# An encoder's feed-forward input projections: one moving operand of 512 columns from the high and low parts of x, halves added afterwards

## The chip, the cores and the metric

The kernel runs on one core of a Trainium2 chip. The metric is the device time of one execution in microseconds, the median of the runs; lower is better. Five engines work in parallel, each through its own queue in order: PE (matrix multiply), DVE (vector), ACT (scalar and activation), POOL and SP (which issues the DMAs here).

## The reference, cut

An encoder of two layers over 256 tokens of 1024 features. Each layer is a mixer (two kinds of attention and a short convolution, gated), a cross attention to a memory of 256 tokens, and a feed-forward part with a convolution over tokens in its gate; each ends in a residual and a layer norm. All is in fp32. The feed-forward part is

```python
def conv_ffn(x, ffn_w_in, ffn_conv_w, ffn_conv_b, ffn_w_out):
    u, gt = jnp.split(x @ ffn_w_in, 2, axis=-1)      # 1024 -> 2 x 2816
    a = dwconv(gt, ffn_conv_w) + ffn_conv_b          # 3 taps over the tokens
    return (jax.nn.silu(a) * u) @ ffn_w_out
```

## The kernel before, in words

Every fp32 product is made of three matmuls on fp32r operands: both factors are split into a high part (ACT casts it) and a low part (DVE subtracts the cast from the source), in `split_from` (L249); `mm3` (L243) multiplies high by high, high by low and low by high into one PSUM bank, so L245, L246 and L247 carry nearly all of PE's time.

The weights come as 355 units of 512 KB. `prefetch` (L1089) brings each by DMA into a `raw` tile and splits it into a `hi` and a `lo` tile of 128x1024, seven units ahead of their use (LOOK); eight pairs of tiles exist (WB). A unit of the input projections holds 8 blocks of 128x128 for one block of 128 output features, and `proj_f8` (L263) runs 8 x 3 matmuls with the weights stationary and 256 tokens of x moving. x lies in four tiles named big, two for high and two for low parts (class `Act`); `ln` fills them at the end of a layer norm: PE transposes x by 128x128 (L414) into a PSUM bank of the kind `att`, and `split_from` splits it.

PSUM has eight banks of 512 columns: three `acc` and five `att`. The feed-forward input, `ffn_in` (L1013), runs over 22 blocks f of 128 features. A block has a unit for up and one for gate; both write one acc bank, columns 0 to 255 and 256 to 511. ACT and DVE then apply the convolution (L1039, L1040, L1042), the silu (L1044) and the product with up (L1045) straight from the bank, and the result is split for `ffn_out`. In layer 1 the up parts of the first four blocks are computed earlier, tokens on the partitions, by `up_first` (L1003), while x's second half is still being normalized; for these blocks (`f < ready`) only a gate unit is run and the stored up is transposed into the same bank (L1029).

`Encoder.interleave` plans the steps of the main chain and the steps that fill its waits; from the planned program a tile scheduler sets the order of the instructions on each engine, so that a change of the instructions can change the order around it. Splits behind a layer norm are marked urgent, and weight splits are held behind them. SP's queue carries the DMAs in program order. In the rows, names are of the program: `hi` and `lo` a unit's weights, `big` the tiles of x or of the memory, `fa` the gate's tile in SBUF, `ident` the identity for a transposition.

Of the kernel before, what the change touches and what calls it, by code (L numbers as in the profile page):

```python
# [20 lines left out]
F32R = mybir.dt.float32r  # L21
# [4 lines left out]
P = 128  # L26
D = 1024
KT = 8
# [57 lines left out]
class Step:  # L86
# [5 lines left out]
    def __init__(self, fn, cost=0.0, lat=0.0, units=(), acq=0, rel=0, fill=0):  # L92
        self.fn, self.cost, self.lat, self.units = fn, cost, lat, list(units)
        self.acq, self.rel, self.fill = acq, rel, fill
# [97 lines left out]
        return self.los[k // self.per][:, k % self.per, a:b]  # L192


def rd(t):
    return t.bitcast(F32)


class Encoder:
# [63 lines left out]
    def proj_f8(self, u, xa, o):  # L263

        hi, lo = (t.rearrange("p (k c) -> p k c", k=KT) for t in u)
        for k in range(KT):
            self.mm3(o, hi[:, k], lo[:, k], xa.hi(k), xa.lo(k), k == 0, k == KT - 1)

    def proj_m2(self, u, xa, kt, i, o, first, last):

# [89 lines left out]
    def ln(self, i, nxt, rel, pre=2.6):  # L360
# [46 lines left out]
        def transp(h):  # L407
            nc, n = self.nc, w // P
            if i == 0 and h == 0:
                self.T[nxt] = self.act_tile()  # L410
            a = self.T[nxt]
            pt = self.att()[:, :w].rearrange("p (k t) -> p k t", k=n)
            for k in range(n):
                nc.tensor.transpose(pt[:, k], self.x[i][:, (n * h + k) * P:(n * h + k + 1) * P], self.ident)  # L414
            t, k = n * h // 4, n * h % 4
            for ins in self.split_from(pt, a.his[t][:, k:k + n, i * P:(i + 1) * P],
                                       a.los[t][:, k:k + n, i * P:(i + 1) * P]):
                self.urgent(ins)

        yield Step(norm, 0, pre, rel=rel)  # L420
# [39 lines left out]
    def load_mem(self, then=None):  # L460

        n = 1024 if then is None else 512
        hi, lo = [self.big(F32R) for _ in range(2)], [self.big(F32R) for _ in range(2)]
        for j in range(2 * 1024 // n):
            raw = self.raw() if then is None else self.t512()
            t = j * n // 1024
            for m in range(0, n, 256 if then is not None and j == 0 else n):
                w = 256 if then is not None and j == 0 else n
                sl = slice(j * n % 1024 + m, j * n % 1024 + m + w)
                self.nc.sync.dma_start(raw[:, m:m + w], self.aps["memT"][:, j * n + m:j * n + m + w])  # L470
                self.split_from(raw[:, m:m + w], hi[t][:, sl], lo[t][:, sl])
                if then is not None:
                    then(j, m)
        self.T["mem"] = Act([t.rearrange("p (k t) -> p k t", k=4) for t in hi],
                            [t.rearrange("p (k t) -> p k t", k=4) for t in lo])

    def raw(self):
        return self.wp.tile([P, 1024], F32, tag="raw", name=self.nm("raw"), bufs=4)
# [534 lines left out]
    def ffn_in(self, l, xn, ready=0):  # L1013
        T = self.T
        for f in range(NF):
            st = {}

            def up(u, f=f, st=st):
                st["o"] = self.acc()
                self.proj_f8(u, T[xn], st["o"][:, 0:256])  # L1020

            def gate(u, f=f, st=st):
                nc = self.nc
                if f < ready:
                    st["o"] = self.acc()
                self.proj_f8(u, T[xn], st["o"][:, 256:512])
                if f < ready:
                    for i in range(NT):
                        nc.tensor.transpose(st["o"][:, i * P:(i + 1) * P], T["um", i][:, f * P:(f + 1) * P],  # L1029
                                            self.ident)  # L1030
                if f == 0:
                    T["hT"] = Act([self.big4(F32R)], [self.big4(F32R)])
                elif f % 4 == 0:
                    T["hT"].his.append(self.big4(F32R))
                    T["hT"].los.append(self.big4(F32R))
                w = self.fcw[:, l, f]
                ug = st["o"].rearrange("p (j t) -> p j t", j=2)
                t = self.tmp.tile([P, S], F32, tag="fa", name=self.nm("fa"), bufs=3)
                nc.scalar.activation(t, ug[:, 1], AF.Identity, bias=w[:, 3:4], scale=w[:, 1:2])  # L1039
                nc.vector.scalar_tensor_tensor(out=t[:, 1:], in0=ug[:, 1, :S - 1], scalar=w[:, 0:1], in1=t[:, 1:],  # L1040
                                               op0=ALU.mult, op1=ALU.add)
                nc.vector.scalar_tensor_tensor(out=t[:, :S - 1], in0=ug[:, 1, 1:], scalar=w[:, 2:3],  # L1042
                                               in1=t[:, :S - 1], op0=ALU.mult, op1=ALU.add)
                nc.scalar.activation(t, t, AF.Silu)  # L1044
                nc.vector.tensor_tensor(out=t, in0=t, in1=ug[:, 0], op=ALU.mult)  # L1045
                self.split_from(t, T["hT"].hi(f), T["hT"].lo(f))
            if f >= ready:
                yield Step(up, U, units=[("fu", l, f)])
            yield Step(gate, U, units=[("fg", l, f)])
# [171 lines left out]
```

## Time and profile before

| | us |
|---|---|
| time, median of 3 runs | 1135.65 (1134.47 to 1135.9) |
| the profiled execution | 1135.06 |
| its span, first to last instruction | 1133.3 |
| PE busy in the span | 1103.8 (97%) |
| DVE busy | 798.9 (70%) |
| ACT busy | 612.7 (54%) |
| granted clock of PE, mean | 0.994 |

The span is one execution seen by the profiler; 1.8 us of the execution's time lie around it. Busy time of PE contains waits that pipelining hides, so the distance between the starts of two matmuls tells more than their durations. The idle time in brackets behind a row of a timeline is that of the engine just before it, and the name behind the arrow is what ended it.

### The profile page before, as it was taken

How to read it: one execution, taken by the hardware profiler on the slowest of the kernel's cores; microseconds unless marked ns; L12 is line 12 of the kernel's file. 1: busy time of each engine (PE TensorE's matmuls, PEld its weight loads, DVE VectorE, ACT ScalarE, POOL GpSimd, SP SyncE). 2: the span in 40 equal slices, each digit the busy share in tenths (PEclk: the TensorE clock that was granted, in tenths of full speed). 3: DMA queues.
4: the chain of work that ended last, by engine and by line, in shares of the span. 5: the costliest groups of instructions: out<-in, count | busy, mean ns of one | idle time of the engine just before them, and what ended most of it. 6: DMA issues, size and time to landing. Idle time of an engine off the chain costs nothing.

```text
span 1133.3 us, 18595 instructions
## 1 busy us (share of the span) xinstructions
PE 1103.8 (97%) x7340; PEld 1014.8 (90%) x7340; DVE 798.9 (70%) x1198; ACT 612.7 (54%) x958; POOL 12.4 (1%) x18
## 2 busy tenths in 40 slices
PE   7999999999999999999999999999999979999997
PEld 6899998888898999998889999888889879999986
DVE  6788888666864876665586888865787576666644
ACT  5556767445453565554445667744536436555540
POOL 0000000000000000000000000000000000000001
PEclk9999999999999999999999999999999989999999
DMA  8785437567563666565747544556746444665551
GB/s 297 245 262 170 136 135 232 183 189 241 168 186 99 200 204 186 182 181 189 263 143 231 174 148 167 179 185 197 256 145 201 140 149 150 186 185 180 182 180 37
DMA packets 60471, 208.53 MB, mean 184 GB/s; under 512 B 7008, under 2 KB 8288, under 8 KB 60384
## 3 DMA queue, kind: packets, MB, share of 16 engines
q1 hardware_dynamic: 59952, 206.83, 56.9%
q8 instruction: 57, 0.93, 0.3%
q10 hardware_dynamic: 432, 0.52, 0.1%
q14 instruction: 30, 0.25, 0.1%
HBM read 204.18 MB, written 1.05 MB: 181 GB/s over the span
## 4 chain that ended last, share of the span: by engine, by line
PE 66%; DVE 3%; ACT 1%; DMA 1%; issue 1%; DVEq 0%; ACTq 0%; SPq 0%
PE acc L245 18%; PE acc L246 18%; PE acc L247 18%; PE att L246 3%; PE att L247 3%; PE att L245 3%; DMA raw<-in_w_dram 1%; DVE lo L251 1%; PE att L414 0%; ACT hi L250 0%; DVE s L355 0%; DVE big L251 0%; PE att L617 0%; PE att L851 0%; PE att L1003 0%
## 5 line engine op out<-in xcount | busy, mean ns | idle before, releaser
L251 DVE TENSOR_TENSOR lo<-raw,hi 128x1024 fp32r<-128x1024 f32 x355 | 431.8, 1222 | 237.1 <-ACT hi L250 235.6
L250 ACT CAST hi<-raw 128x1024 fp32r<-128x1024 f32 x355 | 370.7, 1050 | 333.1 <-PE acc L246 155.5
L245 PE MATMUL acc<-big,hi 128*128 128x256 f32 x1376 | 391.0, 285 | 3.1 <-ACT big L294 1.2
L246 PE MATMUL acc<-big,hi 128*128 128x256 f32 x1376 | 390.2, 284 | 1.9 <-DVE big L251 1.9
L247 PE MATMUL acc<-big,lo 128*128 128x256 f32 x1376 | 390.2, 284 | 0.6 <-DVE lo L251 0.6
L245 PEld LDWEIGHTS acc<-big,hi 128*128 128x128 f32 x1376 | 263.3, 192 | 5.1 <-ACT big L294 1.8
L246 PEld LDWEIGHTS acc<-big,hi 128*128 128x128 f32 x1376 | 263.6, 192 | 3.0 <-DVE big L251 2.6
L247 PEld LDWEIGHTS acc<-big,lo 128*128 128x128 f32 x1376 | 263.6, 192 | 1.2 <-DVE lo L251 1.1
L245 PE MATMUL acc<-hi,big 128*128 128x512 f32 x584 | 230.1, 396 | 6.1 <-ACT hi L250 6.0
L246 PE MATMUL acc<-lo,big 128*128 128x512 f32 x584 | 230.8, 395 | 0.5 <-DVE lo L251 0.5
L247 PE MATMUL acc<-hi,big 128*128 128x512 f32 x584 | 228.0, 393 | 0.0
L245 PEld LDWEIGHTS acc<-hi,big 128*128 128x128 f32 x584 | 110.5, 190 | 27.1 <-ACT hi L250 6.5
L247 PEld LDWEIGHTS acc<-hi,big 128*128 128x128 f32 x584 | 110.7, 190 | 23.0
L246 PEld LDWEIGHTS acc<-lo,big 128*128 128x128 f32 x584 | 110.9, 190 | 21.2 <-DVE lo L251 1.2
L246 PE MATMUL att<-lo,big 128*128 128x256 f32 (+1 forms) x228 | 72.6, 319 | 0.0
L245 PE MATMUL att<-hi,big 128*128 128x256 f32 (+1 forms) x228 | 72.4, 318 | 0.0
L247 PE MATMUL att<-hi,big 128*128 128x256 f32 (+1 forms) x228 | 72.3, 318 | 0.0
L250 ACT CAST big<-att 128x512 fp32r<-128x512 f32 (+2 forms) x64 | 28.1, 458 | 45.8 <-PE att L247 25.8
L251 DVE TENSOR_TENSOR big<-att,big 128x512 fp32r<-128x512 f32 (+2 forms) x64 | 32.1, 518 | 27.7 <-ACT big L250 27.2
L245 PEld LDWEIGHTS att<-hi,big 128*128 128x128 f32 x228 | 43.3, 190 | 4.9
L246 PEld LDWEIGHTS att<-lo,big 128*128 128x128 f32 x228 | 43.3, 190 | 4.5
L247 PEld LDWEIGHTS att<-hi,big 128*128 128x128 f32 x228 | 43.3, 190 | 3.1
(145 smaller groups left out, 948.2 us busy)
## 6 DMA issues: line engine op xcount, KB each, us to landing
raw<-in_w_dram SPq DMA_DIRECT2D x355, 512.0 KB, 4.0
t<-in_bias_dram SPq DMA_DIRECT2D x16, 256.0 KB, 5.5
big<-in_ln_g_dram SPq DMA_DIRECT2D x6, 512.0 KB, 5.5
big<-in_ln_b_dram SPq DMA_DIRECT2D x6, 512.0 KB, 6.2
raw<-in_memT_dram SPq DMA_DIRECT2D x6, 512.0 KB, 4.4
big<-big SPq DMA_DIRECT2D x16, 128.0 KB, 2.3
x<-in_x_dram SPq DMA_DIRECT2D x4, 256.0 KB, 7.9
t<-in_memT_dram SPq DMA_DIRECT2D x3, 256.0 KB, 7.9
```

The lines of the kernel that those rows point to most:

```text
L245: mm(o, lh, rh, start=first, stop=False)
L246: mm(o, lh, rl, start=False, stop=False)
L247: mm(o, ll, rh, start=False, stop=last)
L250: return (self.nc.scalar.copy(ah, src), self.nc.vector.tensor_tensor(out=al, in0=src, in1=rd(ah), op=ALU.subtract))
L251: self.nc.vector.tensor_tensor(out=al, in0=src, in1=rd(ah), op=ALU.subtract))
```

## The change

The tiles of x behind every layer norm, and those of the memory, get a new layout (class `Twin`): each of the four tiles holds two blocks of 128 features, for each the 256 tokens of the high part and beside them the 256 of the low part. Splits are made two blocks at a time, so a transposition of 512 columns takes two casts and two subtractions where it took one of each.

In the feed-forward input, `proj_twin` takes the place of `proj_f8`: with a high weight stationary it moves high and low part of x in one matmul of 512 columns, and with a low weight the high part alone, 256 columns. The first wide matmul opens the bank, the eight with low weights follow in one run, then the other seven wide ones. The bank's two halves must be added: `fold` copies the second half to SBUF on ACT and adds the first on DVE. So up and gate have a bank each, which is free after the fold, and convolution and product read SBUF. In layer 1's first four blocks the transposed up goes to an acc bank of its own, which the product reads.

```diff
+class Twin:
+    def __init__(self, tiles):
+        self.tiles = [t.rearrange("p (k h t) -> p k h t", k=2, h=2) for t in tiles]
+    def hi(self, k, a=0, b=S):
+        return self.tiles[k // 2][:, k % 2, 0, a:b]
+    def lo(self, k, a=0, b=S):
+        return self.tiles[k // 2][:, k % 2, 1, a:b]
+    def both(self, k):
+        return self.tiles[k // 2][:, k % 2].rearrange("p h t -> p (h t)")
+    def put(self, split, src, k, a=0, b=S):
+        out, n = [], src.shape[1]
+        for j in range(k, k + n, 2):
+            m = min(2, n)
+            t = self.tiles[j // 2][:, j % 2:j % 2 + m]
+            got = split(src[:, j - k:j - k + m], t[:, :, 0, a:b], t[:, :, 1, a:b])
+            out += got or ()
+        return out
...
+    def proj_twin(self, u, xa):
+        mm, o = self.nc.tensor.matmul, self.acc()
+        hi, lo = (t.rearrange("p (k c) -> p k c", k=KT) for t in u)
+        mm(o, hi[:, 0], xa.both(0), start=True, stop=False)
+        for k in range(KT):
+            mm(o[:, S:], lo[:, k], xa.hi(k), start=False, stop=False)
+        for k in range(1, KT):
+            mm(o, hi[:, k], xa.both(k), start=False, stop=k == KT - 1)
+        return o
+    def fold(self, dst, o):
+        self.nc.scalar.copy(dst, o[:, S:])
+        self.nc.vector.tensor_tensor(out=dst, in0=o[:, :S], in1=dst, op=ALU.add)
...
-                self.T[nxt] = self.act_tile()
+                self.T[nxt] = Twin([self.big(F32R) for _ in range(4)])
...
-            t, k = n * h // 4, n * h % 4
-            for ins in self.split_from(pt, a.his[t][:, k:k + n, i * P:(i + 1) * P],
-                                       a.los[t][:, k:k + n, i * P:(i + 1) * P]):
+            for ins in a.put(self.split_from, pt, n * h, i * P, (i + 1) * P):
                 self.urgent(ins)
...
             def up(u, f=f, st=st):
-                st["o"] = self.acc()
-                self.proj_f8(u, T[xn], st["o"][:, 0:256])
+                st["ug"] = self.t512().rearrange("p (j t) -> p j t", j=2)
+                self.fold(st["ug"][:, 0], self.proj_twin(u, T[xn]))
+                st["up"] = st["ug"][:, 0]
...
                 if f < ready:
-                    st["o"] = self.acc()
-                self.proj_f8(u, T[xn], st["o"][:, 256:512])
+                    st["ug"] = self.t512().rearrange("p (j t) -> p j t", j=2)
+                self.fold(st["ug"][:, 1], self.proj_twin(u, T[xn]))
                 if f < ready:
+                    st["up"] = self.acc()[:, 0:256]
                     for i in range(NT):
-                        nc.tensor.transpose(st["o"][:, i * P:(i + 1) * P], T["um", i][:, f * P:(f + 1) * P],
+                        nc.tensor.transpose(st["up"][:, i * P:(i + 1) * P], T["um", i][:, f * P:(f + 1) * P],
...
-                ug = st["o"].rearrange("p (j t) -> p j t", j=2)
+                ug = st["ug"]
...
-                nc.vector.tensor_tensor(out=t, in0=t, in1=ug[:, 0], op=ALU.mult)
+                nc.vector.tensor_tensor(out=t, in0=t, in1=st["up"], op=ALU.mult)
```

`load_mem` fills a `Twin` in the same way, through `put`. The line numbers of the changed file are higher by 26 to 41: `split_from` stands on L276 and L277, `proj_twin` on L299 to L303, `fold` on L307 and L308, the transposition of up on L1067.

PE, one unit of layer 0's feed-forward input in the steady part, before (the first 6 of 24 matmuls):

```order
L245 MATMUL acc_4183<-big_3930,hi_3955 128x256
L246 MATMUL acc_4183<-big_3932,hi_3955 128x256
L247 MATMUL acc_4183<-big_3930,lo_3956 128x256
L245 MATMUL acc_4183<-big_3930,hi_3955 128x256
L246 MATMUL acc_4183<-big_3932,hi_3955 128x256
L247 MATMUL acc_4183<-big_3930,lo_3956 128x256
```

and in the changed program (the whole unit; x2 is two matmuls of the same row):

```order
L299 MATMUL acc_4428<-big_3941,hi_4211 128x512 [waits DVE_49]
L301 MATMUL acc_4428<-big_3941,lo_4212 128x256 x2
L301 MATMUL acc_4428<-big_3942,lo_4212 128x256 x2
L301 MATMUL acc_4428<-big_3943,lo_4212 128x256 x2
L301 MATMUL acc_4428<-big_3944,lo_4212 128x256 x2
L303 MATMUL acc_4428<-big_3941,hi_4211 128x512
L303 MATMUL acc_4428<-big_3942,hi_4211 128x512 x2
L303 MATMUL acc_4428<-big_3943,hi_4211 128x512 x2
L303 MATMUL acc_4428<-big_3944,hi_4211 128x512 x2
```

24 matmuls became 16, those with the low weights stand together behind the first, and the unit waits for DVE (its bank).

PE, layer 1, between the gates of the second and the third block (t is the stored up), before:

```order
L247 MATMUL acc_9925<-big_9739,lo_9651 128x256
L1029 MATMUL acc_9925<-ident,t_9837 128x128
L1029 MATMUL acc_9925<-ident,t_9874 128x128
L245 MATMUL acc_9966<-big_9738,hi_9662 128x256
L246 MATMUL acc_9966<-big_9740,hi_9662 128x256
L247 MATMUL acc_9966<-big_9738,lo_9663 128x256
```

and in the changed program, at the same place:

```order
L303 MATMUL acc_9738<-big_9553,hi_9462 128x512 x2
L1067 MATMUL acc_9757<-ident,t_9653 128x128 [waits DVE_49]
L1067 MATMUL acc_9757<-ident,t_9690 128x128
L299 MATMUL acc_9775<-big_9550,hi_9474 128x512 [waits DVE_49]
L301 MATMUL acc_9775<-big_9550,lo_9475 128x256 x2
L301 MATMUL acc_9775<-big_9551,lo_9475 128x256 x2
```

The transposed up went to the gate's own bank and now goes to another, for which it waits, and the next gate waits for a bank too.

DVE, layer 0, where x is split for the cross attention's query projection (att: the transposed x; big_288 and big_289: the memory's keys), before:

```order
L251 TENSOR_TENSOR lo_3075<-raw_3072,hi_3074 128x1024 [waits DMAHW6_49,Activation_49]
L251 TENSOR_TENSOR lo_3113<-raw_3110,hi_3112 128x1024 [waits DMAHW7_49,Activation_49]
L251 TENSOR_TENSOR big_3050<-att_3141,big_3048 128x2x128 [waits Activation_49]
L251 TENSOR_TENSOR lo_3149<-raw_3146,hi_3148 128x1024 [waits DMAHW0_49,Activation_49]
L251 TENSOR_TENSOR big_3195<-big_289,big_3193 128x1024 [waits Activation_49]
L251 TENSOR_TENSOR big_3050<-att_3177,big_3048 128x2x128 [waits Activation_49]
L251 TENSOR_TENSOR big_3051<-att_3182,big_3049 128x2x128 [waits Activation_49]
L251 TENSOR_TENSOR big_3051<-att_3187,big_3049 128x2x128 [waits Activation_49]
```

and in the changed program:

```order
L277 TENSOR_TENSOR lo_3085<-raw_3082,hi_3084 128x1024 [waits DMAHW6_49,Activation_49]
L277 TENSOR_TENSOR big_3058<-att_3113,big_3058 128x2x128 [waits Activation_49]
L277 TENSOR_TENSOR big_3056<-att_3153,big_3056 128x2x128 [waits Activation_49]
L277 TENSOR_TENSOR big_3057<-att_3189,big_3057 128x2x128 [waits Activation_49]
L277 TENSOR_TENSOR big_3058<-att_3194,big_3058 128x2x128 [waits Activation_49]
L277 TENSOR_TENSOR big_3059<-att_3199,big_3059 128x2x128 [waits Activation_49]
L277 TENSOR_TENSOR big_3059<-att_3113,big_3059 128x2x128 [waits Activation_49]
L277 TENSOR_TENSOR lo_3125<-raw_3122,hi_3124 128x1024 [waits DMAHW7_49,Activation_49]
L277 TENSOR_TENSOR lo_3161<-raw_3158,hi_3160 128x1024 [waits DMAHW0_49,Activation_49]
L277 TENSOR_TENSOR big_3206<-big_288,big_3204 128x1024 [waits Activation_49]
```

One weight split (`lo` from `raw`) stands ahead of x's pieces where two stood, the pieces of x follow one another, and the splits from big_288 and big_289 come behind them.

## Rows read from the trace of the kernel before

**Rows 1.** The page: engines (busy us, share of span, instructions); the chain that ended last.

```profile
PE 1103.8 (97%) x7340; PEld 1014.8 (90%) x7340; DVE 798.9 (70%) x1198; ACT 612.7 (54%) x958; POOL 12.4 (1%) x18
...
PE 66%; DVE 3%; ACT 1%; DMA 1%; issue 1%; DVEq 0%; ACTq 0%; SPq 0%
```

**Rows 2.** The page, costliest groups: busy us, mean ns of one, idle time before.

```profile
L245 PE MATMUL acc<-big,hi 128*128 128x256 f32 x1376 | 391.0, 285 | 3.1 <-ACT big L294 1.2
...
L245 PEld LDWEIGHTS acc<-big,hi 128*128 128x128 f32 x1376 | 263.3, 192 | 5.1 <-ACT big L294 1.8
```

**Rows 3.** Timeline of PE, layer 0, feed-forward: start us, duration us, line, operation.

```profile
439.79 0.28 PE L245 MATMUL acc<-big,hi 128*128 128x256 f32 x1
...
442.67 0.28 PE L245 MATMUL acc<-big,hi 128*128 128x256 f32 x1
```

**Rows 4.** Windows: us, busy of PE, PEld, DVE, ACT, POOL, PEclk, DMA, GB/s.

```profile
440.00:460.00 20.00, 20.00 (x169) 20.00 (x168) 13.83 (x22) 11.16 (x19) 0.00 (x0) 1.00 0.59 184
300.00:304.00 4.00, 2.36 (x18) 1.88 (x18) 4.00 (x7) 3.26 (x7) 0.00 (x0) 1.00 0.20 36
928.00:932.00 4.00, 1.50 (x7) 1.53 (x8) 4.00 (x10) 0.68 (x2) 0.00 (x0) 0.50 0.75 252
```

**Rows 5.** Timeline of PE, layer 0, where 512 and 256 columns are mixed.

```profile
519.89 0.40 PE L245 MATMUL acc<-hi,big 128*128 128x512 f32 x1
520.12 0.40 PE L246 MATMUL acc<-lo,big 128*128 128x512 f32 x1
520.36 0.39 PE L247 MATMUL acc<-hi,big 128*128 128x512 f32 x1
...
521.73 0.39 PE L247 MATMUL att<-hi,big 128*128 128x512 f32 x1
521.96 0.28 PE L245 MATMUL att<-hi,big 128*128 128x256 f32 x1
...
522.67 0.40 PE L245 MATMUL acc<-hi,big 128*128 128x512 f32 x1
```

**Rows 6.** Timeline of ACT, first feed-forward blocks of layer 1.

```profile
954.65 1.28 ACT L1044 ACT_TABLE_LOAD   x1
955.94 0.42 ACT L1044 ACTIVATE fa<-fa 128x256 f32<-128x256 f32 x1
...
957.20 0.40 ACT L250 CAST big<-fa 128x256 fp32r<-128x256 f32 x1
```

**Rows 7.** Timeline of DVE, same stretch.

```profile
956.39 0.42 DVE L1045 TENSOR_TENSOR fa<-fa,acc 128x256 f32<-128x256 f32 x1 [0.57 <-ACT fa L1044]
956.73 0.48 DVE L1042 SCALAR_TENSOR_TENSOR fa<-acc,fcw,fa 128x255 f32<-128x255 f32 x1
```

**Rows 8.** Timeline of PE, same stretch (in brackets: idle before, released by).

```profile
956.08 0.38 PE L1029 MATMUL acc<-ident,t 128*128 128x128 f32 x2
956.87 0.39 PE L245 MATMUL acc<-big,hi 128*128 128x256 f32 x1 [0.40 <-DVE fa L1045]
```

**Rows 9.** Timeline of PE at three starts behind a layer norm.

```profile
301.65 0.62 PE L245 MATMUL acc<-big,hi 128*128 128x256 f32 x3 [0.29 <-ACT big L250]
...
303.84 0.39 PE L246 MATMUL acc<-big,hi 128*128 128x256 f32 x1 [1.35 <-DVE big L251]
...
306.44 0.39 PE L246 MATMUL acc<-big,hi 128*128 128x256 f32 x1 [0.20 <-DVE big L251]
...
387.25 0.62 PE L245 MATMUL acc<-big,hi 128*128 128x256 f32 x3 [0.33 <-ACT big L250]
...
930.50 1.09 PE L414 MATMUL att<-ident,x 128*128 128x128 f32 x4 [6.20 <-DVE x L378]
```

**Rows 10.** Timeline of DVE at the first of them.

```profile
301.10 2.35 DVE L251 TENSOR_TENSOR lo<-raw,hi 128x1024 fp32r<-128x1024 f32 x2
303.37 0.42 DVE L251 TENSOR_TENSOR big<-att,big 128x256 fp32r<-128x256 f32 x1
```

More of the change, by code (lines that the diff above doesn't have):

```diff
@@ L462, in load_mem @@
         n = 1024 if then is None else 512
-        hi, lo = [self.big(F32R) for _ in range(2)], [self.big(F32R) for _ in range(2)]
+        mem = Twin([self.big(F32R) for _ in range(4)])
         for j in range(2 * 1024 // n):
             raw = self.raw() if then is None else self.t512()
-            t = j * n // 1024
             for m in range(0, n, 256 if then is not None and j == 0 else n):
                 w = 256 if then is not None and j == 0 else n
-                sl = slice(j * n % 1024 + m, j * n % 1024 + m + w)
                 self.nc.sync.dma_start(raw[:, m:m + w], self.aps["memT"][:, j * n + m:j * n + m + w])
-                self.split_from(raw[:, m:m + w], hi[t][:, sl], lo[t][:, sl])
+                mem.put(self.split_from, raw[:, m:m + w].rearrange("p (k t) -> p k t", t=S), (j * n + m) // S)
                 if then is not None:
                     then(j, m)
-        self.T["mem"] = Act([t.rearrange("p (k t) -> p k t", k=4) for t in hi],
-                            [t.rearrange("p (k t) -> p k t", k=4) for t in lo])
+        self.T["mem"] = mem
     def raw(self):
```

## The prediction, made before the run

> **What bounds the kernel now.** The engine table comes first [rows 1]: PE is busy 97% of the span, DVE 70%, ACT 54%, and two thirds of the chain that ended last is PE. So the end moves with PE's work and with the few places where PE stands still. The costliest groups [rows 2] say what that work is: 128x256 matmuls, 1376 on L245 and as many on L246 and L247; the weight loads beside them (0.19 us) are hidden, since the matmuls follow one another in less. Their own duration (0.28 us) is latency: what one costs is the distance between two starts. In the feed-forward part [rows 3] that is 0.12 us without a gap: a unit starts at 439.79, the next, 24 matmuls later, at 442.67, so 2.88 us. All through those stretches PE is 20.00 of 20 us busy at clock 1.00, DVE 13.83, ACT 11.16 [rows 4]: nothing waits. A unit is worth its PE time there, as long as nothing new waits.
>
> **Part 1: fewer, longer matmuls.** Each changed unit replaces 24 matmuls of 256 columns by 8 of 512 (x's high part and low part beside each other, under the same high weights) and 8 of 256. The columns are the same, so the gain is whatever a matmul costs beyond its columns. Elsewhere the kernel runs 128x512 matmuls mixed with 128x256 ones, like the new unit [rows 5]: from 519.89 to 521.73 eight starts apart take 1.84 us (0.23 each), and the six of 256 columns from 521.96 take 0.71 us to 522.67, so eight take 0.95. A unit becomes 1.84 + 0.95 = 2.79 us, 0.09 less. There are 84 such units (2 x 22 in layer 0, 18 up and 22 gate in layer 1): **−7.5 us**, and I take −7.4. Bounds: with 0.24 for two of the eight wide ones (520.12 to 520.36 is such a gap) and 0.12 for each narrow one a unit is 6 x 0.23 + 2 x 0.24 + 0.96 = 2.82 and the gain 5.0 us; with 0.228 for the wide ones (520.36 to 521.73 are six gaps) and 0.95 for the narrow ones it is 2.77 and the gain 9.2. The Trainium skill, "TensorE: Matmul & The Clock Gate", section "Wait — 56ns, not 53.3ns?", gives start-to-start as columns over 2.4 GHz plus about 2.5 ns; by that the estimate of the gain is 84 x 8 x 2.5 ns = 1.7 us only. The rows disagree: two of 256 columns take 0.24, one of 512 takes 0.23 or less, 10 to 12 ns a pair. It is a rival below.
>
> **Part 2: the additions.** Each unit now ends in an ACT copy of one half of the bank to SBUF and a DVE addition. Nearest rows: an ACT pass over 128x256 takes 0.40 us [rows 6], a DVE pass of that shape that reads PSUM 0.42 [rows 7], in a queue about 0.34 each. DVE's work for a unit was 13.83 / 20 x 2.88 = 1.99 us and becomes some 2.36 of 2.79 (85%), ACT's 1.61 becomes 1.95 (70%). Both fit. The next wait they could cause is PE's for an accumulation bank: there are three, one unit each, so the addition has until the end of the second unit after, 5.6 us. Ahead of it in DVE's order stand at most one weight split (1.22), two convolution steps, a product and a split of 0.4 to 0.5 each: some 2.9 us. So the additions cost nothing in the steady part; if that cover were gone they would cost up to 0.8 us a unit.
>
> **Part 3: layer 1's first four blocks.** Here no up unit lies between the gates, because up was computed earlier; the transposed up goes now to a bank of its own, held until the product at the end of the block. Three banks serve gate, up, gate, up, and each new unit must wait for something that was not in its way before. Before, the third gate waited once, 0.40 us, for the product of the first block [rows 8]; that product is late because ACT loads a table (1.28 us) ahead of the silu [rows 6]. I walk the new order from these times. The second gate's matmuls end near 952.75, its transposes follow. The third gate needs the second's bank: drain of the last matmul (0.16, its 0.28 or so less one start), copy 0.40, addition 0.42, two hand-overs of 0.06 (the product ends at 956.81, PE starts at 956.87 [rows 7, 8]): stall **1.07**. The fourth gate, wanted at 956.9, needs the bank of the second block's up, so that block's product. Behind the table load come the first silu, its product (956.42), on DVE two steps of 0.48 for the second block, a silu of 0.41 and the product of 0.42: ready 958.48, stall **1.58**. The fifth block's up, wanted at 961.4, needs the fourth gate's bank, so copy and addition again: **1.0**. Then two units a block return and the slack with them. Sum 3.65, less the 0.40 that goes: **+3.25 us**. Bounds: 2.0, if the last of the three has passed before PE comes, and 5.0, if one weight split of 1.22 us stands ahead of an addition. The clock is no further cost: an idle stretch of 1.35 us left it at 1.00, 6.2 us of idle time were followed by 0.50 [rows 4, 9].
>
> **Part 4: the starts behind a layer norm.** All layer-norm outputs take the new layout, and a transposition of 512 columns is split in two pieces: one more instruction on ACT and one on DVE, twice a layer norm, about 0.16 us each, all before the other token half's norm and in DVE time that is not yet waited for. But the scheduler's order shifts. At layer 0's cross-attention query projection PE waits 0.29 and 1.35 us [rows 9], because the low part of x (303.37) stands behind two weight splits (301.10 to 303.45) on DVE [rows 10]. In the changed order one split stands ahead and the memory's split has moved behind the four pieces of x: the low part is ready some 1.2 to 1.5 us sooner, and the three pieces behind follow at once. Of 1.84 us of idle time there (0.29, 1.35, and 0.20 at 306.44) I take **−1.5**; bounds 0 and −1.84. At layer 0's feed-forward start PE waits 0.33 us for ACT [rows 9]; there the first unit's second matmul now needs all the columns of both halves, and the last transposition waits for a split to free its bank: **+0.2**, bounds 0 and 0.8. The remaining starts (mixer, layer 1's query projection) change their order by a piece or two in either direction: 0, bounds −1 and +1.
>
> **Sum.** −7.4 + 3.25 − 1.5 + 0.2 = −5.45 on the profiled execution's 1135.06: 1129.6. The median of the runs, 1135.65, stands 0.6 above it, so **1130.1** for the median.
>
> **The rivals.**
> A: a 512-column matmul costs two of 256. For it: single gaps of 0.24 in rows 5, twice 0.12. Against it: the run of eight takes 1.84, not 1.92. Gain 0, the other terms stay: 1135.65 + 1.95 = 1137.6; with the page's 1.7 us, 1135.9.
> B: the banks cost more at layer 1's start, because an addition stands behind a weight split each time and the waits feed on one another (each late product delays the next gate, whose addition is then later): 3 x 1.22 more than the walk, 7 us. For it: DVE is in order and splits are 1.22. Against it: the order puts two of the additions before the split. 1130.1 + 3.7 = 1133.8.
> C: the walk is too dark: ACT and DVE get ahead there, one stall of the three stays, 1.0 less the 0.40. 1130.1 − 2.6 = 1127.5, with the best bound of part 1 1125.7.
> D, slower than before: DVE becomes the bound of the steady part. Its 2.36 us a unit would have to stretch past 2.88, by 22%, through PSUM reads that PE, ACT and DVE share or through waits for silu that block it in order. From there every 0.1 us a unit is 8.4 us: at 2.98 the part loses 8.4 instead of gaining 7.4, 1130.1 + 15.8 = 1145.9. Against it: DVE runs now at 69% there without such stretching, its splits at 1.22 as anywhere.
>
> **How the numbers follow.** Forecast 0.56, C 0.17, B 0.13, A 0.06, D 0.04, other shifts of order 0.04. The range: the bounds of part 1 (−9.2, −5.0) with those of part 3 (2.0, 5.0) and part 4 reach from 1125.6 to 1137.4; leaving out 2 in 10, half on each side, gives 1126.3 to 1134.6. A measurement here can tell about 0.2% (2.3 us) from no change, so faster means under 1133.4: the forecast nearly whole, C, and a part of B: 0.78. Within 0.2%: the rest of B, most of A and of the shifts: 0.14. Slower, over 1137.9: D, the dark part of A, and a part of the shifts: 0.08.
>
> **What would show it.** Right: in the feed-forward stretches the first matmuls of successive units 2.77 to 2.82 us apart, PE 20 of 20 us busy, DVE near 17 and ACT near 14; three idle times of PE of 1.0 to 1.6 us near 950 to 960, put down to DVE's addition and product; one idle time at 302 under 0.5 us. Wrong: units at 2.88 (A), PE idle at the start of units with DVE full (D), idle time at 950 to 960 of 6 us or more (B) or 1 us (C), or new waits at a place that the walk left at nothing, the mixers' starts above all.

## The result and the profile after

The changed kernel takes 1126.68 us, median of 4 runs (1125.99 to 1127.0); the kernel before, in 4 runs beside it, 1135.11 (1134.47 to 1135.9). The ratio is 0.9933, interval 0.9917 to 0.9949: faster by 0.7%. The forecast was 1130.1, its range 1126.3 to 1134.6. The time lies inside, 0.4 us above the range's lower end.

The page of the changed kernel, engines and chain (columns as in [rows 1]):

```profile
PE 1094.9 (97%) x6668; PEld 978.2 (87%) x6668; DVE 833.2 (74%) x1300; ACT 643.4 (57%) x1060; POOL 12.4 (1%) x18
...
PE 92%; DVE 3%; ACT 2%; DMA 1%; issue 1%; SPq 0%; DVEq 0%; ACTq 0%
```

PE has 8.9 us less work, DVE 34 more, ACT 31 more, and the span (1125.1 us) is 8.1 shorter. In the feed-forward part of layer 0 the timeline of PE reads (an entry with x8 is eight matmuls; start us, us, line, operation):

```profile
440.95 0.39 PE L299 MATMUL acc<-big,hi 128*128 128x512 f32 x1
441.18 1.11 PE L301 MATMUL acc<-big,lo 128*128 128x256 f32 x8
442.13 1.78 PE L303 MATMUL acc<-big,hi 128*128 128x512 f32 x7
443.75 0.39 PE L299 MATMUL acc<-big,hi 128*128 128x512 f32 x1
```

From one unit's first matmul to the next it is 2.80 us, and over 40 units in a row 2.793 (they start within 0.002 us of that), where [rows 3] show 2.88. The stretch from 440 to 460 us, columns as in [rows 4]:

```profile
440.00:460.00 20.00, 20.00 (x115) 17.56 (x114) 16.44 (x28) 13.80 (x26) 0.00 (x0) 1.00 0.62 192
```

PE still waits for nothing there, with DVE at 16.44 of 20 us and ACT at 13.80.

The span can be cut where x's first transposition stands behind each layer norm (lines L414 before, L455 after). The lengths of these stages, worked out from the starts of those rows and of the last matmul (the first stage counts from PE's first matmul, 4.5 to 4.7 us into the span), for the kernel before, the changed one, its repetition on another chip, and four experiments told of below:

| stage, us | before | after | again | e4 | e7 | e3 | e1 |
|---|---|---|---|---|---|---|---|
| start to first layer norm | 23.97 | 23.56 | 21.74 | 22.04 | 22.38 | 21.95 | 23.19 |
| mixer, layer 0 | 263.91 | 263.86 | 263.89 | 263.92 | 263.92 | 263.91 | 264.04 |
| cross attention, layer 0 | 90.63 | 88.48 | 88.49 | 88.50 | 89.03 | 88.49 | 88.49 |
| feed-forward, layer 0 | 194.13 | 190.43 | 190.43 | 193.88 | 194.15 | 190.43 | 193.96 |
| mixer, layer 1 | 261.59 | 261.07 | 261.07 | 261.06 | 261.29 | 261.06 | 261.09 |
| cross attention, layer 1 | 91.68 | 91.45 | 91.44 | 91.45 | 91.67 | 91.44 | 91.44 |
| feed-forward, layer 1 | 194.24 | 193.25 | 193.30 | 194.38 | 194.11 | 189.85 | 197.79 |

The middle stages of the changed kernel repeat to 0.03 us, so differences of 0.2 us there are the program's. The first stage differs by 2 us between executions, whatever the kernel, and the traces show with what: in the profiles of before, after and e1 (23.97, 23.56, 23.19) a stretch between 11 and 17 us of the span has a granted clock of 0.50, in the four others (21.74 to 22.38) none has.

Layer 1's first blocks, PE's timeline (in brackets the idle time before, and what ended it):

```profile
945.21 0.38 PE L1067 MATMUL acc<-ident,t 128*128 128x128 f32 x2
946.29 0.50 PE L299 MATMUL acc<-big,hi 128*128 128x512 f32 x1 [0.70 <-DVE t L308]
...
949.21 0.38 PE L1067 MATMUL acc<-ident,t 128*128 128x128 f32 x2
951.01 0.50 PE L299 MATMUL acc<-big,hi 128*128 128x512 f32 x1 [1.42 <-DVE fa L1083]
...
953.92 0.38 PE L1067 MATMUL acc<-ident,t 128*128 128x128 f32 x2
955.01 0.50 PE L299 MATMUL acc<-big,hi 128*128 128x512 f32 x1 [0.70 <-DVE t L308]
```

Three units start late, as the walk had it: each first matmul stands 1.08, 1.80 and 1.09 us behind the start of the first of two transpositions (the row marked x2), where 0.14 is the distance without a wait (as in e3 below, 943.86 to 944.00). So the waits are 0.94, 1.66 and 0.95 us. In [rows 8] the one wait is 0.65 by the same measure (956.08 to 956.87). The idle times that the profile gives are shorter: 0.70, 1.42 and 0.70, and 0.40 before. ACT at that place:

```profile
945.41 0.37 ACT L307 COPY t<-acc 128x256 f32<-128x256 f32 x1 [1.21 <-PE acc L303]
...
946.75 1.28 ACT L1082 ACT_TABLE_LOAD   x1
948.04 0.42 ACT L1082 ACTIVATE fa<-fa 128x256 f32<-128x256 f32 x1
...
950.08 0.42 ACT L1082 ACTIVATE fa<-fa 128x256 f32<-128x256 f32 x1 [0.73 <-DVE fa L1080]
```

and DVE:

```profile
945.81 0.42 DVE L308 TENSOR_TENSOR t<-acc,t 128x256 f32<-128x256 f32 x1
...
948.49 0.42 DVE L1083 TENSOR_TENSOR fa<-fa,acc 128x256 f32<-128x256 f32 x1 [0.50 <-ACT fa L1082]
...
950.53 0.42 DVE L1083 TENSOR_TENSOR fa<-fa,acc 128x256 f32<-128x256 f32 x1 [0.21 <-ACT fa L1082]
```

The copy of a gate's half (945.41) is followed by the addition (945.81, ends 946.23) and that by PE (946.29); the middle wait is the one for the second block's product (950.53), behind table load, silu, and the next block's silu.

### The profile page after: what moved, and what is told of

It reads as the page before. It is cut to its first block, busy times and chain, and to the rows that moved or that the text cites. A ratio compares the mean times of both kernels' runs of the same rounds, so it can differ in the third digit from the quotient of the medians.

```text
span 1125.1 us, 17377 instructions
## 1 busy us (share of the span) xinstructions
PE 1094.9 (97%) x6668; PEld 978.2 (87%) x6668; DVE 833.2 (74%) x1300; ACT 643.4 (57%) x1060; POOL 12.4 (1%) x18
## 4 chain that ended last, share of the span: by engine, by line
PE 92%; DVE 3%; ACT 2%; DMA 1%; issue 1%; SPq 0%; DVEq 0%; ACTq 0%
PE acc L272 18%; PE acc L271 18%; PE acc L273 18%; PE acc L303 12%; PE acc L301 7%; PE att L272 4%; PE att L273 4%; PE att L271 4%; PE acc L299 2%; DVE lo L277 1%; DMA raw<-in_w_dram 1%; PE att L455 1%; PE att L653 1%; PE att L568 1%; DVE x L414 1%
## 5 line engine op out<-in xcount | busy, mean ns | idle before, releaser
L277 DVE TENSOR_TENSOR lo<-raw,hi 128x1024 fp32r<-128x1024 f32 x355 | 432.2, 1223 | 186.9 <-ACT hi L276 180.7
L276 ACT CAST hi<-raw 128x1024 fp32r<-128x1024 f32 x355 | 371.4, 1051 | 223.5 <-PE acc L273 75.3
L271 PE MATMUL acc<-big,hi 128*128 128x256 f32 x704 | 200.3, 285 | 3.2 <-ACT big L335 2.4
L273 PE MATMUL acc<-big,lo 128*128 128x256 f32 x704 | 200.5, 285 | 0.8 <-DVE lo L277 0.8
L272 PE MATMUL acc<-big,hi 128*128 128x256 f32 x704 | 200.0, 284 | 0.2 <-DVE big L277 0.2
L303 PE MATMUL acc<-big,hi 128*128 128x512 f32 x588 | 149.2, 393 | 0.0
L271 PEld LDWEIGHTS acc<-big,hi 128*128 128x128 f32 x704 | 134.6, 191 | 4.4 <-ACT big L335 2.8
L273 PEld LDWEIGHTS acc<-big,lo 128*128 128x128 f32 x704 | 134.8, 191 | 1.2 <-DVE lo L277 1.1
L272 PEld LDWEIGHTS acc<-big,hi 128*128 128x128 f32 x704 | 134.8, 191 | 0.8 <-DVE big L277 0.4
L303 PEld LDWEIGHTS acc<-big,hi 128*128 128x128 f32 x588 | 105.1, 189 | 18.3
L301 PEld LDWEIGHTS acc<-big,lo 128*128 128x128 f32 x672 | 91.9, 190 | 6.7 <-ACT big L276 0.2
L301 PE MATMUL acc<-big,lo 128*128 128x256 f32 x672 | 94.1, 282 | 0.0
L307 ACT COPY t<-acc 128x256 f32<-128x256 f32 x84 | 31.2, 372 | 65.1 <-PE acc L303 65.1
```

Of the source, the lines that this page charges most:

```text
L271: mm(o, lh, rh, start=first, stop=False)
L272: mm(o, lh, rl, start=False, stop=False)
L273: mm(o, ll, rh, start=False, stop=last)
L276: return (self.nc.scalar.copy(ah, src), self.nc.vector.tensor_tensor(out=al, in0=src, in1=rd(ah), op=ALU.subtract))
L277: self.nc.vector.tensor_tensor(out=al, in0=src, in1=rd(ah), op=ALU.subtract))
L301: mm(o[:, S:], lo[:, k], xa.hi(k), start=False, stop=False)
```

## The experiments

Ratios are against the kernel before in the same job; its medians differ from chip to chip (1132.5 to 1135.1 us), so single times aren't compared across jobs.

**What the wide matmuls are worth.** The gain of the unit was put to the test by cutting seven of eight wide matmuls in two again, with all else kept:

```diff
         for k in range(1, KT):
-            mm(o, hi[:, k], xa.both(k), start=False, stop=k == KT - 1)
+            mm(o[:, :S], hi[:, k], xa.hi(k), start=False, stop=False)
+            mm(o[:, S:], hi[:, k], xa.lo(k), start=False, stop=k == KT - 1)
```

> The changed kernel, with seven of a unit's eight wide matmuls cut into two of 256 columns again (one under the high part of x, one under the low part, into the same two halves of the bank); layout, banks and additions stay. Theory (what a matmul costs beyond its columns is paid once less): a unit goes from 2.793 us to 0.23 + 22 x 0.12 = 2.87, 84 units give +6.5 us, so about 1133.2. Rival (the gain came from the shifted order of work around the layer norms, and the width of the matmuls is worth 2.5 ns each): units at most 0.02 us longer, +1.5 us, so 1126.7 to 1128.2.

1132.84 us, ratio 0.9987 (0.9974 to 1.0000), so 0.5% above the changed kernel's ratio. PE's timeline, one unit:

```profile
442.42 0.40 PE L299 MATMUL acc<-big,hi 128*128 128x512 f32 x1
442.66 1.12 PE L301 MATMUL acc<-big,lo 128*128 128x256 f32 x8
443.61 0.28 PE L303 MATMUL acc<-big,hi 128*128 128x256 f32 x1
443.73 0.29 PE L304 MATMUL acc<-big,hi 128*128 128x256 f32 x1
...
445.29 0.40 PE L299 MATMUL acc<-big,hi 128*128 128x512 f32 x1
```

A unit takes 2.87 us, every matmul of 256 columns 0.12. Layer 0's feed-forward stage is 3.53 us longer than after, 0.080 a unit for seven pairs: 11.5 ns a pair. The rival is out: the layout and its order, kept here, don't make the units shorter. Each matmul has a weight load of its own (6668 of each on the page of the changed kernel), so a merged pair saves a matmul and a load; which of the two the 11.5 ns belong to, no run here tells.

**Does the run of low-weight matmuls matter?** They were put one behind each wide matmul:

```diff
         for k in range(KT):
-            mm(o[:, S:], lo[:, k], xa.hi(k), start=False, stop=False)
-        for k in range(1, KT):
-            mm(o, hi[:, k], xa.both(k), start=False, stop=k == KT - 1)
+            if k:
+                mm(o, hi[:, k], xa.both(k), start=False, stop=k == KT - 1)
+            if k < KT - 2:
+                mm(o[:, S:], lo[:, k], xa.hi(k), start=False, stop=False)
+            if k == KT - 2:
+                for j in (k, k + 1):
+                    mm(o[:, S:], lo[:, j], xa.hi(j), start=False, stop=False)
```

> The changed kernel, with the matmuls under low weights no longer in one run but one behind each wide matmul (the last two together, ahead of the last wide one). Theory (only the number of matmuls counts): a unit stays at 2.77 to 2.80 us, so 1125.5 to 1127.5. Rival (the run is part of the gain, each change of width costs some 10 ns as the gaps of 0.24 behind narrow matmuls in the kernel before could say): 13 changes more a unit, 0.13 us, 84 units, +11 us, so about 1137.

1128.62 us, ratio 0.9963 (0.9950 to 0.9976). Neither expectation was right. The timeline of PE:

```profile
441.02 0.40 PE L299 MATMUL acc<-big,hi 128*128 128x512 f32 x1
441.25 0.28 PE L304 MATMUL acc<-big,lo 128*128 128x256 f32 x1
441.37 0.40 PE L302 MATMUL acc<-big,hi 128*128 128x512 f32 x1
441.60 0.28 PE L304 MATMUL acc<-big,lo 128*128 128x256 f32 x1
...
443.84 0.40 PE L299 MATMUL acc<-big,hi 128*128 128x512 f32 x1
```

A unit takes 2.82 us, against 2.793 with the run: the wide matmuls take 0.23 to 0.24 behind a narrow one. So the run is worth 0.027 us a unit, 2.2 us in all: nearly a third of the units' gain hangs on the order, a fifth of what the rival said.

**Layer 1's three waits.** The transposed up of the first four blocks goes to an att bank:

```diff
-                    st["up"] = self.acc()[:, 0:256]
+                    st["up"] = self.att()[:, 0:256]
```

> The changed kernel, with the transposed up of layer 1's first four blocks in a bank of the five att ones instead of the three acc ones. Theory (PE's three idle times of 0.91, 1.62 and 0.91 us between these blocks are a lack of acc banks): at least the second and third go, a unit's bank is then free two blocks later; 3.4 us less, so about 1123.3. Rival (the waits are for the late silu behind the table load, whatever the bank): they move to other instructions of the same blocks and the time stays at 1126.0 to 1126.7.

1123.06 us, ratio 0.9910 (0.9895 to 0.9925): the lowest ratio of all kernels here. PE's timeline:

```profile
940.87 0.47 PE L299 MATMUL acc<-big,hi 128*128 128x512 f32 x1
...
943.86 0.38 PE L1067 MATMUL att<-ident,t 128*128 128x128 f32 x2
944.00 0.48 PE L299 MATMUL acc<-big,hi 128*128 128x512 f32 x1
...
947.02 0.48 PE L299 MATMUL acc<-big,hi 128*128 128x512 f32 x1
...
950.04 0.48 PE L299 MATMUL acc<-big,hi 128*128 128x512 f32 x1
```

The units now start 3.13, 3.02 and 3.02 us apart, two transpositions among them, and no idle time is left. The stage is 3.40 us shorter than after. The lack of acc banks is shown as the cause; the table load comes 23.6 us behind the first transposition of the stage as it did 23.4 us behind it in after, and nobody waits for it.

**What the layout does by itself.** Tiles and split as in the change, the feed-forward input as in the kernel before (`proj_f8`, one bank for up and gate).

> The layout alone: x and the memory in the new tiles with their split into pieces, and the feed-forward input as in the kernel before (24 matmuls a unit, one bank for up and gate, no addition). The units gain 7.27 us in the change (84 x 0.0866) and the bank waits cost 2.8; the measured 8.4 leave 3.9 us for the rest. Theory (that rest is the layout's, by another order of the splits on DVE and ACT at the starts behind layer norms): about 1131.2. Rival (only the query projection's 2.2 us in layer 0 is the layout's, what is left is a matter of the single execution): 1132.9. Second rival (the rest comes with the additions and freed banks): 1135.1.

1129.65 us, ratio 0.9973 (0.9964 to 0.9983). That is 3.1 us below the kernel before, with an interval of 1.9 to 4.1, so the time alone does not part the first theory (3.9 us) from the rival of 2.2; the stages do: they show more than the rival's one place. The table has 2.13 us in layer 0's cross attention, 0.53 and 0.23 in layer 1's mixer and cross attention, all three as in after, and 0.25 in layer 0's feed-forward part with its old units; layer 1's feed-forward part is 0.14 longer. So the layout alone brings some 3 us; what is left of the theory's 3.9 is the start and the low clock of one execution, as the rival had it. That the layout does so through the order of the splits is shown for one stage by the next run; for the others it is argued.

**The query projection.** The kernel before, with only the keys' split held behind x's split:

```diff
-            self.split_from(src[t], hi[t], lo[t])
+            for ins in self.split_from(src[t], hi[t], lo[t]):
+                self.behind(ins)
```

> The kernel before with one thing of the changed order: the two splits of the memory's keys (1.22 us each on DVE) are held behind the split of x, as weight splits are. Theory (at layer 0's query projection PE waited 1.35 us because x's normalization and split came late on DVE, and the keys' split ahead of them is one cause): 1.1 to 1.6 us less in the stage from x's transposition to the next layer norm, nothing elsewhere in layer 0. Rival (only the weight split that no longer stands ahead in the changed order counts): no change in that stage.

1132.71 us, ratio 0.9984 (0.9970 to 0.9998); the stage went from 90.63 to 89.03. In the kernel before, one of the two splits stood ahead of the normalization on DVE:

```profile
296.59 1.23 DVE L251 TENSOR_TENSOR big<-big,big 128x1024 fp32r<-128x1024 f32 x1
297.73 1.67 DVE L373 SCALAR_TENSOR_TENSOR x<-x,s,big 128x256 f32<-128x256 f32 x4
```

DVE in this kernel, which has no such split there:

```profile
296.66 1.67 DVE L378 SCALAR_TENSOR_TENSOR x<-x,s,big 128x256 f32<-128x256 f32 x4
298.25 2.35 DVE L251 TENSOR_TENSOR lo<-raw,hi 128x1024 fp32r<-128x1024 f32 x2
300.52 0.42 DVE L251 TENSOR_TENSOR big<-att,big 128x256 fp32r<-128x256 f32 x1
```

and PE:

```profile
298.87 1.03 PE L414 MATMUL att<-ident,x 128*128 128x128 f32 x8
...
300.99 0.39 PE L246 MATMUL acc<-big,hi 128*128 128x256 f32 x1 [0.39 <-DVE big L251]
```

The two weight splits still stand ahead of x's split, as in [rows 10]; but x was ready sooner, since the keys' split no longer stands ahead of the normalization itself, and of the 1.35 us of [rows 9] 0.39 is left. In the changed kernel one weight split has gone too:

```profile
296.94 1.67 DVE L419 SCALAR_TENSOR_TENSOR x<-x,s,big 128x256 f32<-128x256 f32 x4
298.53 1.22 DVE L277 TENSOR_TENSOR lo<-raw,hi 128x1024 fp32r<-128x1024 f32 x1
299.67 0.42 DVE L277 TENSOR_TENSOR big<-att,big 128x256 fp32r<-128x256 f32 x1
```

```profile
300.03 1.03 PE L455 MATMUL att<-ident,x 128*128 128x128 f32 x8
301.14 0.62 PE L271 MATMUL acc<-big,hi 128*128 128x256 f32 x3
301.60 0.39 PE L272 MATMUL acc<-big,hi 128*128 128x256 f32 x1
```

The piece at 299.67 waits for nothing behind the normalization, and PE has no idle time left worth a bracket. So of the 2.15 us in this stage 1.60 are the keys' split; the other 0.55 is what the remaining reordering gives (the weight split is its likely part, not tried by itself). Of the 0.53 us in layer 1's mixer this run has 0.30 (261.29 against 261.59).

**The cover of the additions.** The addition made twice, then three times (the extra ones into a tile that nothing reads):

```diff
     def fold(self, dst, o):
         self.nc.scalar.copy(dst, o[:, S:])
+        for s in self.spare[:1]:        # [:2] in the second
+            self.nc.vector.tensor_tensor(out=s, in0=o[:, :S], in1=dst, op=ALU.add)
         self.nc.vector.tensor_tensor(out=dst, in0=o[:, :S], in1=dst, op=ALU.add)
```

> The changed kernel with the addition of a unit's halves made twice on DVE (the first into a tile that nothing reads). DVE has 2.30 us of work a unit in the steady part now (16.44 of 20 us, units of 2.793) and gets 0.33 to 0.42 more, so 2.63 to 2.72. Theory (the additions are covered as long as DVE's work stays under PE's 2.79): units stay at 2.793 us, the time grows by under 1 us (some of the waits at layer 1's first blocks get 0.35 longer). Rival (DVE in order, with its waits for the silu, loses the cover before it is full): units of 2.85 us or more, 5 us or more.

> As e6_add_twice, with the addition made three times: 2.96 to 3.14 us of DVE's work a unit. Theory: DVE becomes the bound, units of 2.96 to 3.14 us, so 14 to 29 us more than the changed kernel (84 units). Rival (accumulation banks and prefetched weights even it out): under 5 us more.

1127.93 us, ratio 0.9961 (0.9946 to 0.9976), and 1137.76 us, ratio 1.0042 (1.0025 to 1.0059). The stretch from 440 to 460 us of the one and the other:

```profile
440.00:460.00 20.00, 20.00 (x116) 17.58 (x115) 18.69 (x38) 13.29 (x24) 0.00 (x0) 1.00 0.62 190
440.00:460.00 20.00, 20.00 (x118) 17.66 (x118) 20.00 (x43) 13.72 (x25) 0.00 (x0) 1.00 0.62 185
```

With DVE at 18.69 of 20 us the steady units still take 2.793 us. The cost, 1.28 us in layer 0's feed-forward stage and 0.65 in layer 1's, lies at their starts, where DVE still works off what the layer norm has held up: the third unit of layer 0 starts 3.97 us ahead of the fourth, and of layer 1's three waits the first and the third are 0.55 us longer, the second 0.55 shorter. So the cover held, and the price of 1.9 us was more than the 1 us that the theory allowed. With the third addition DVE is full, and even so 28 units in a row keep 2.79 us in layer 0; the predicted units of 2.96 us and more did not come, and neither expectation was right. DVE's lag (0.31 us an addition by the first stretch, so 2.92 us of work a unit) seems to be carried along, since weights are split seven units ahead, and the scheduler put matmuls of `ffn_out` between the last units; this was not taken further. But the two stages are 2.6 and 7.8 us longer, and the kernel is slower than before. That is not yet rival D of the prediction, whose price came in each unit. Here it came at the starts: in layer 0 two waits (1.28 and 0.79 us), in layer 1 two of 2.99 us, where after had 0.70, 1.42 and 0.70, and behind them a lower clock:

```profile
964.08 0.76 PE L299 MATMUL acc<-big,hi 128*128 128x512 f32 x1 [2.99 <-DVE t L310]
```

```profile
963.00:970.00 7.00, 5.92 (x19) 5.08 (x20) 3.34 (x9) 2.14 (x6) 0.00 (x0) 0.52 0.28 99
```

Over the trace (from 30 to 1100 us) PE works 14.0 us at a granted clock of 0.50, in after 3.0. Half of such time is lost, by an estimate from the transpositions in the last section, so some 5.5 us of what this kernel is longer is the clock's.

**More units the same way.** On top of e3, the wide matmuls for the 40 units of qa, ka, gc and the memory's keys (the addition in the place of the copy), for all 88 remaining units, and for the 16 of the keys alone. The core of the first is

```diff
     def feat_copy(self, n, l, xn):
...
+                self.fold(self.T[n][:, i], self.proj_twin(u, self.T[xn]))
```

> The changed kernel with up's transposition in an att bank (as in e3_att_bank), and the same wide matmuls for the 40 further units whose result is only copied out of the bank: qa, ka, gc (4 units each and layer) and the memory's keys (8 each layer); the addition takes the place of the copy. Theory (0.087 us a unit wherever PE is the bound): 3.5 us less than e3_att_bank, so 13.5 us less than the kernel before. Rival (in the mixers DVE is the later engine and the bank is freed later, behind DVE's queue): no gain or a loss against e3_att_bank.

> As e5_copies_too, and also the remaining 48 units with stationary weights (hc, gb, qb, kb, the cross attention's query), whose halves are added into an SBUF tile that the old reading instructions then read. Theory: 4.2 us less again, 17.7 less than the kernel before. Rival (DVE pays 0.35 us more a unit where it is already waited for, and the results are some 0.8 us later in chains that PE waits for: the query projection ahead of the heads): less than 2 us of it, or a loss against e5_copies_too.

> As e3_att_bank, with the wide matmuls also for the 16 units of the memory's keys alone, which fill PE's waits in the attention parts; qa, ka and gc as in the kernel before. Theory (what e5_copies_too lost came from the chains behind qa, ka and gc; the keys have nobody waiting for them soon): 16 x 0.087 = 1.4 us less than e3_att_bank, 11.5 us less than the kernel before. Rival (any further unit with a fold shifts the order of the splits at the starts): 1 to 5 us more than e3_att_bank.

1133.86 us, ratio 0.9993 (0.9978 to 1.0009); 1146.23 us, ratio 1.0102 (1.0072 to 1.0132); 1129.13 us, ratio 0.9959 (0.9943 to 0.9974). All three lose against e3 (0.9910), by some 9, 22 and 6 us, so the three theories fail; the rivals had a loss. Where the keys alone are changed, layer 0's mixer becomes 266.22 us long, its cross attention 89.57 and its feed-forward part 194.37; these lengths hold fills moved from stage to stage too, for layer 1's cross attention gets 3.4 us shorter. One place of it, PE and DVE at the query projection:

```profile
304.04 0.38 PE L271 MATMUL acc<-big,hi 128*128 128x256 f32 x1 [2.70 <-DVE big L308]
```

```profile
302.45 1.21 DVE L277 TENSOR_TENSOR big<-big,big 128x1024 fp32r<-128x1024 f32 x1
303.58 0.41 DVE L308 TENSOR_TENSOR big<-acc,big 128x256 f32<-128x256 f32 x1
```

PE waits 2.70 us for a bank: the addition of a key unit (303.58) stands on DVE behind two weight splits and the keys' split (302.45). Here a unit whose bank is free only after an addition is no filler, because DVE is busy with a layer norm; this is the reading of one row and was not tried by itself.

The traces show what the three losses consist of. PE's idle stretches (those above 0.15 us, from 30 to 1100 us) add up to 18.4, 29.2 and 15.7 us, in e3 to 10.6; and PE works 15.9, 21.8 and 8.4 us at a granted clock of 0.50, in e3 3.5. Counting half of the latter as lost (an estimate), the waits cost 7.7, 18.6 and 5.0 us, the lower clock 6.2, 9.1 and 2.5, and the wide matmuls give back 3.5, 7.6 and 1.4: in sum 10.4, 20.1 and 6.1, where the spans are 10.7, 20.9 and 7.2 us longer than e3's. So the wide matmuls gave back less than the waits took, and the clock behind the waits made a third to nearly a half of what waits and clock took together. Which chains made each wait was not taken apart.

The changed kernel was also run once more beside these:

> The changed kernel once more, on the chip of the next three. Theory (stages behind the first layer norm repeat to some 0.1 us, only the first 28 us and the time at which PE's clock comes back behind the layer norm of layer 1's feed-forward part differ between executions): 0.9925 to 0.994 of the kernel before, the same stage times as in the first profile of it but for these two. Rival (the smaller differences of stages, 0.53 us in layer 1's mixer and 0.23 in its cross attention, are chance): they are gone or of the other sign.

1125.47 us, ratio 0.9927 (0.9901 to 0.9952), the stages as in the table's column "again". The small gains of layer 1 are there again, to 0.01 us, so the rival is out.

## Why the prediction was right, and by how much not

The sign, the likeliest case and the mechanism held; the gain was 2.9 us larger than forecast (5.5 against the median shown then, 8.4 measured). The other 0.5 us between 1130.1 and 1126.68 is the kernel before, which took 1135.11 beside the changed one and not 1135.65. (The sum itself gives 1130.2; 1130.1 is a slip.) It still lies in the range because that took in the good bounds of all parts: parts 1 to 3 came within 0.4 us each, while the starts behind the layer norms gained some 1.5 us more than forecast, and most of the rest of the 2.9 is the start and the clock of single executions.

- **Part 1, the units, −7.4:** 84 x (2.88 − 2.793) = −7.3, and e1 gives 11.5 ns a pair where rows 3 and 5 gave 10 to 12. The Trainium skill's fixed cost of about 2.5 ns ("TensorE: Matmul & The Clock Gate", "Wait — 56ns, not 53.3ns?") would have given 1.7; for these operands, with a new weight load for each matmul, the trace disagrees with it. That the low-weight matmuls stand in one run is 2.2 us of the gain (e2). The walk did not ask for this; the rows that it used had runs of either width, like the new unit, so it did no harm.
- **Part 2, the additions, 0:** right. DVE reached 16.44 of 20 us (82%, forecast 85), and one addition more does not lengthen the steady units.
- **Part 3, layer 1's start, +3.25:** measured by the starts, three waits of 0.94, 1.66 and 0.95 us against one of 0.65 before, so +2.9 (the expectations above count each 0.03 us shorter). The walk had 1.07 (its parts as listed add up to 1.10), 1.58 and 1.0, and the releasers are the ones it named: addition, product, addition. Its sum of 3.65 was right to 0.1; what it took away for the old wait, 0.40, was the profile's idle time, while the stalls were distances between starts. e3 takes 3.4 us away.
- **Part 4, the query projection, −1.5:** the stage gained 2.15, above the bound of 1.84. The step looked at the splits ahead of x's low part; e7 shows that the larger part was one step earlier, the keys' split ahead of x's normalization. The idle time that a profile puts down at one wait is no bound where a new order also moves what comes before it.
- **Part 4, the feed-forward start, +0.2:** the stage became 3.70 us shorter, and its 44 units are 44 x (2.880 − 2.793) = 3.8 of it, so some +0.1 is left at the start, as forecast. PE does wait ahead of the last transposition, 0.48 us for a split on DVE, and the first unit takes 3.16 us instead of 2.79. The 0.25 that the layout gains in this stage by e4 holds for the old units alone.
- **Part 4, the remaining starts, 0:** this is the term that failed most beside the query projection. Layer 1's mixer gained 0.52 and its cross attention 0.23, both with the layout alone (e4 has them, the repetition too); 0.30 of the first comes by holding back the keys' split (e7).
- **Outside the steps:** the start was 0.4 us shorter in this execution, which is chance (21.7 to 24.0 in the table), and layer 1's feed-forward stage spent 3.0 us at the low clock instead of 4.1 (last section).

Sum by the table: −0.4 − 0.05 − 2.15 − 3.70 − 0.52 − 0.23 − 0.99 = −8.0, of the span's 8.1. Of the rivals, A fell by the units of 2.793 us and by e1, B and C by the three waits that came as walked. D did not come: DVE was at 82%, and even with DVE full (e6_add_thrice) the steady units kept 2.79 us. No run shows the shared PSUM reads that D names: DVE's passes from PSUM took 0.42 us in either kernel.

One sign was set too high: the prediction looked for idle times of 1.0 to 1.6 us near 950, and the profile's are 0.70, 1.42 and 0.70, since the waits were walked as distances.

## What to carry to other kernels

Where PE is the bound and the same weights serve two operands, lay these beside each other and move them in one matmul: here each pair saved some 11 ns, and the addition of the halves cost nothing in the steady part, because DVE had room (82% after). Count banks wherever a unit now needs its own: the one place that had three for four cost 2.9 us, and another pool gave it back. A layout that cuts splits into smaller pieces changes the scheduler's order at every start, and that was worth 3 us here. And look at the clock where a change adds waits: when more units were done this way, new waits and the lower clock behind them took some 7 to 28 us (the estimate above), and the units gained 1.4 to 7.6.

## What the runs showed of the hardware beside this

PE's clock after the long wait. Behind the layer norm ahead of layer 1's feed-forward part PE stands idle for 6.2 to 6.5 us in all kernels here ([rows 9] has 6.20). When it resumes its granted clock is at the lower of its levels (0.50, so 1.2 GHz), and transpositions start 0.213 us apart, where it is 0.11 at 1.00. How long it stays there differs between executions of nearly the same work: up to 4.1 us behind the first transposition in the kernel before, 3.0 and 3.1 in the two of the changed one, 6.1 and 6.0 in e1 and e2. Windows of the changed kernel (two) and of e1 (two; its first transposition starts at 926.81), columns as in [rows 4]:

```profile
923.40:926.40 3.00, 3.00 (x15) 3.00 (x15) 3.00 (x9) 0.74 (x2) 0.00 (x0) 0.50 0.37 142
926.40:930.00 3.60, 3.60 (x26) 3.16 (x25) 2.32 (x7) 1.80 (x4) 0.00 (x0) 1.00 0.00 0
925.00:929.00 4.00, 2.19 (x11) 2.23 (x12) 4.00 (x12) 0.67 (x2) 0.00 (x0) 0.50 0.64 239
929.00:933.00 4.00, 4.00 (x18) 3.81 (x18) 2.62 (x7) 0.75 (x2) 0.00 (x0) 0.51 0.02 4
```

By the 0.213 and 0.11 half of that time is lost, so 3.1 us more at the low clock move the stage by some 1.5 us: in e1 the first unit starts 13.82 us behind the first transposition, in after 12.36. That is the rest of the 4.5 us by which e1's last stage is longer than after, where 40 units at 0.080 explain 3.2.

Shorter waits went both ways. Waits of 1.35 us in the kernel before [rows 9], of 1.42 us in after and of 2.17 us in e5_all_units left the granted clock at 1.00; 2.70 us in e8_keys_too and 2.99 us, twice, in e6_add_thrice were followed by 0.50. At layer 0's feed-forward start e5_copies_too and e8_keys_too have the same two waits, 0.88 and 1.5 us; 0.50 followed in the one, 1.00 stayed in the other. So the length of a wait alone does not tell here what the clock does.
